# A hybrid decoder layer on one core: ten gate stripes behind the attention projections, and a recurrence's second half in three slots

## The chip, the cores and the metric

The kernel runs on one core of a Trainium2 chip. The metric is the device time of one execution in microseconds, the median of a few runs. TensorE multiplies, VectorE (DVE), ScalarE (ACT) and GpSimd (POOL) work on tiles in on-chip memory, and SyncE (SP) issues every DMA of the kernel. Each engine takes its instructions in the order in which the program wrote them.

## The reference, cut to what matters

One layer for a prompt of 1024 tokens and 8 single sample tokens, 1032 columns in all, in f32:

```
xn   = rms_norm(x, norm_pre)
u, z_rnn, q, k, v, z_attn, g_rnn, g_attn = split(xn @ w_in)      # w_in: 1024 x 9216
uc   = causal_conv(u, width 4)
r, i = sigmoid(uc @ w_a + b_a), sigmoid(uc @ w_x + b_x)           # 16 blocks of 64
a    = exp(-8 r softplus(-lambda));  b = sqrt(1 - a^2) * i * uc
h_t  = a_t h_(t-1) + b_t
y_rnn  = (h * silu(z_rnn)) @ w_rnn_out
o_g, lse_g = dilated_window_attention(q_g, k_g, v_g)              # 3 groups x 8 heads of 64
y_attn = (softmax-weighted sum of o_g * silu(z_attn)) @ w_attn_out
out  = x + rms_norm((sigmoid(g_rnn) y_rnn + sigmoid(g_attn) y_attn) @ w_out, norm_post)
```

The new convolution rows, recurrent states and keys and values are outputs too.

## The kernel before, in words

Channels lie on the 128 partitions and tokens along the row. An f32 product is made of three passes over values split into a high and a low part (`mm3`): ACT rounds the high part, DVE subtracts to get the low one. A **stripe** is 128 output channels for all 1032 tokens: four chunks of 256 to 264 columns, 8 blocks of input channels, three passes, 96 matmuls (`project`). A **pair** makes two stripes at once by a scheme of seven block products in place of eight (`project_pair`): 7 products x 2 halves x 4 blocks x 3 passes of 260 columns, with sums and differences of the weight blocks made on the fly (`pair_pieces`) and the results added up on DVE (L639). When a pair's results are complete, a close (`later(2500, ...)`, L661 and L666) copies or activates them and sends them to DRAM.

The order of the stages: norm and the first eight stripes (`FIRST`); sixteen pairs (`PAIRS`: inputs u, gates g and z, a, values v); then for four head pairs and three groups the stripes of keys and queries, with attention run between them; then eight gate stripes (`LATE_GATES`); then the output products. The last two gate stripes are written only when all merging and sampling has been written (the `until` in the loop over the late gates); `split_ya` (L1412) then splits the attention result for the next product.

What is written between the matmuls is decided by a plan. It keeps a clock `clk` in ns that only matmuls advance (a 256-column pass counts 256/2.25 + 4 ns; vector and scalar work and DMAs count nothing). Generators in named **lanes** yield a delay; `tick`, called each half chunk, runs a lane's next step when its due time is past. `later(delay, fn)` puts a call in a queue. `force` jumps the clock to the next due step where something must be finished. So delays are not waits on the chip: they set where in each engine's order an instruction stands.

Tiles come from an arena of 45 slots (`Arena`), handed out in the order in which they were freed. A slot may be freed as soon as the DMA that reads it is written; the next user then waits on the chip for that DMA. A `Room` takes a number of slots for itself. A weight load or a sample's cache load goes ahead only with some slots to spare.

The recurrence has a first half for each of eight blocks (`lru_front`: convolution and gates, run in lane `lru` beside the pairs, in a room of five slots), which stores two tiles to DRAM, and a second half (`lru_back`: loads them, tanh, exp and square root on ACT, products on DVE and POOL, a scan on DVE, the product with z on POOL, a store). The second halves run beside attention in two lanes, `lru` and `lru2`, with a room of four slots each. `attention(g, hp)` has six steps `STEP` = 3400 apart; `merge(hp)` combines the three groups by way of DRAM (L1247, L1253) and POOL (L1262 to L1267); `sample(hp)` attends for the 8 sample tokens.

Of the kernel before, what the change touches and what calls it, by code (L numbers as in the profile page):

```python
# [28 lines left out]
NSLOT = 45  # L29
WARM, WARM_STEP = 46, 7  # L30
GATES = [(kind, b) for kind in range(2) for b in range(8)]
LATE_GATES = 8


FIRST = [("u", 0), ("u", 1), ("g", 0), ("g", 1), ("z", 0), ("z", 1), ("u", 2), ("u", 3)]
PAIRS = [("u", 4), ("g", 2), ("u", 6), ("z", 2), ("v", 0), ("g", 4), ("v", 4), ("z", 4), ("v", 8), ("g", 6),
         ("a", 0), ("z", 6), ("v", 2), ("a", 2), ("v", 6), ("v", 10)]

HALF = 520
OPS = 4  # L40
STEP = 3400
SPARE = 5
KY, VY = 3000, 4000
SLOPES = [[2.0 ** (-8.0 * (g * 8 + h + 1) / 24.0) for h in range(8)] for g in range(3)]
# [52 lines left out]
def hybrid_step(ctx: ExitStack, tc: tile.TileContext, I, O):  # L97
# [10 lines left out]


    MODES = {"wide": {"pj": (0, 1, 2, 3), "s": (4, 5, 6), "o": (7,)},  # L110
             "pair": {"c": (0, 2, 6), "s": (4, 5)},
             "attention": {"pj": (0, 1), "pt": (2, 3), "s": (4, 5, 6), "o": (7,)}}
    mode, turns = ["wide"], {}
    banks = psum.tile([128, 8, 512], F32, name="banks")
# [12 lines left out]
    def later(delay, fn):  # L127
        waiting.append((clk[0] + delay, fn))
# [491 lines left out]
    def project_pair(close, last=False):  # L620

        i = W.use_pair()
        ta = new([128, 2, HALF], F32, "qa")
        quarter = lambda t, q: t[:, q].rearrange("p (c n) -> p c n", c=2)
        c11, c22 = quarter(ta, 0), quarter(ta, 1)
        for step, (wname, xname) in enumerate(STEPS):
            w = W.op(i, wname)
            if step == 1:
                tb = new([128, 2, HALF], F32, "qb")
                c21, c12 = quarter(tb, 0), quarter(tb, 1)  # L630
            p2 = ps_tile("c", 2)[:, :, :HALF // 2]
            for c in range(2):
                for k in range(4):
                    x = x_op(xname, k)[:, :, HALF // 2 * c:HALF // 2 * (c + 1)]
                    mm3(p2[:, c], w[:, 0, k], w[:, 1, k], x[:, 0], x[:, 1], k == 0, k == 3)
                    if k % 2:
                        W.work()
                        yield None
            add = lambda to, by: nc.vector.tensor_tensor(to, p2, by, op=OP.add)  # L639
            if step == 0:  # L640
                nc.scalar.activation(c11, p2, AF.Copy)
            elif step == 1:
                add(c12, c11)
            elif step == 2:
                add(c21, c12)
            elif step == 3:
                add(c12, c12)
                add(c22, c21)
            elif step == 4:
                add(c11, c11)  # L650
            elif step == 5:
                add(c21, c21)
            else:
                add(c12, c12)
            yield None
            W.drop(i, wname)
            if last and step == 3:
                for k in range(4):
                    ar.free(SX.pop(("s1", k)))
                spawn("sums", x21_back())  # L660
            if step == 4:  # L661
                later(2500, lambda: close(((0, 0, ta[:, 0]), (1, 1, ta[:, 1])), ta))
        W.pieces.pop(i)
        W.ops.pop(i)
        W.made.pop(i)
        later(2500, lambda: close(((0, 1, tb[:, 0]), (1, 0, tb[:, 1])), tb))  # L666

    def leave(dst, quarters, t, width=NT, then=None):

# [217 lines left out]
    def lru_front(b):  # L887

        while ("u", b) not in kept_uz:
            yield 1000  # L890
        L = room["L"]
        e, r, x = L(0, [128, EXT]), L(1, [128, CV]), L(2, [128, NT])
        lw = lws.pop(b) if b else load_lw(0)
        nc.sync.dma_start(e[:, 3:3 + SEQ], ud[b])
        nc.gpsimd.memset(e[:, 0:3], 0.0)
        nc.gpsimd.tensor_copy(e[:, SEQ + 6:EXT:4], us[:, b])
        nc.gpsimd.tensor_copy(e[:, SEQ + 3:].rearrange("p (b j) -> p b j", j=4)[:, :, 0:3],
                              par[:, b, 8:32].rearrange("p (b j) -> p b j", j=3))
        yield 6000
        lw = lw.rearrange("p s g c -> p (s g c)")  # L900
        lh = small.tile([128, 256], F32R, tag="lh", name="lh", bufs=1)
        ll = low_w[0]
        nc.scalar.activation(lh, lw, AF.Copy)
        for q in range(2):
            rows, ws = slice(64 * q, 64 * q + 64), slice(128 * q, 128 * q + 128)
            nc.vector.tensor_tensor(ll[rows, ws], lw[rows, ws], f32(lh[rows, ws]), op=OP.subtract)
        nc.scalar.activation(r, e[:, 0:CV], AF.Identity, scale=pcol(b, 0), bias=pcol(b, 4))
        yield 1000
        nc.vector.scalar_tensor_tensor(r, e[:, 1:1 + CV], pcol(b, 1), r, op0=OP.mult, op1=OP.add)
        nc.vector.scalar_tensor_tensor(r, e[:, 2:2 + CV], pcol(b, 2), r, op0=OP.mult, op1=OP.add)  # L910
        yield 3000
        nc.vector.scalar_tensor_tensor(x[:, :SEQ], e[:, 3:3 + SEQ], pcol(b, 3), r[:, :SEQ], op0=OP.mult, op1=OP.add)
        nc.vector.scalar_tensor_tensor(x[:, SEQ:], e[:, SEQ + 6:EXT:4], pcol(b, 3), r[:, SEQ + 3:CV:4],
                                       op0=OP.mult, op1=OP.add)
        nc.gpsimd.tensor_copy(cst[:, b, 0:3], e[:, SEQ:SEQ + 3])
        nc.gpsimd.tensor_copy(cst[:, b, 3:11], e[:, SEQ + 6:EXT:4])
        yield 2500
        xs = [L(q, [128, NT], F32R) for q in range(2)]
        a, t = L(3, [128, NT]), L(4, [128, NT])
        for q in range(2):  # L920
            rows, other = slice(64 * q, 64 * q + 64), slice(64 - 64 * q, 128 - 64 * q)
            nc.scalar.activation(xs[q][rows], x[rows], AF.Copy)
            nc.vector.tensor_tensor(xs[q][other], x[rows], f32(xs[q][rows]), op=OP.subtract)
        yield 4000
        if b + 1 < KB:
            load_lw(b + 1)
        yield 4500
        for q in range(2):
            rows = slice(64 * q, 64 * q + 64)
            ws = slice(128 * q, 128 * q + 128)  # L930
            for c0, n in CHUNKS:
                p = ps_tile("s")
                cs = slice(c0, c0 + n)
                mm(p[:, :n], lh[:, ws], xs[q][:, cs], start=True, stop=False)
                mm(p[:, :n], ll[:, ws], xs[q][:, cs], start=False, stop=True)
                for gate in range(2):
                    at = 64 * (gate ^ q)
                    nc.scalar.activation((a, t)[gate][rows, cs], p[at:at + 64, :n], AF.Sigmoid,  # L938
                                         bias=par[rows, b, 5 + gate:6 + gate])
                yield 1800  # L940
        nc.gpsimd.tensor_tensor(x, x, t, op=OP.mult)
        yield 6000
        nc.sync.dma_start(rxd[b, 0], a)
        nc.sync.dma_start(rxd[b, 1], x)

    def lru_back(b, own):
        L = room[own]
        L.shrink(4)
        a, x, t, s = (L(j, [128, NT]) for j in range(4))
        nc.sync.dma_start(a, rxd[b, 0])  # L950
        nc.sync.dma_start(x, rxd[b, 1])
        yield 8000
        nc.scalar.activation(t, a, AF.Tanh, scale=spk[:, 0, b:b + 1])
        nc.scalar.activation(a, a, AF.Exp, scale=spk[:, 1, b:b + 1])
        nc.scalar.activation(s, t, AF.Sqrt)
        yield 5000
        nc.vector.scalar_tensor_tensor(t, a, 1.0, t, op0=OP.add, op1=OP.mult)
        yield 2000
        nc.vector.tensor_scalar(t, t, -1.0, 1.0, op0=OP.mult, op1=OP.add)
        yield 2000  # L960
        nc.vector.scalar_tensor_tensor(s, t, 1.0, s, op0=OP.add, op1=OP.mult)
        yield 2500
        nc.gpsimd.tensor_tensor(s, s, x, op=OP.mult)
        z = L(0, [128, NT])
        nc.sync.dma_start(z, zd[b])
        yield 5000
        nc.vector.tensor_tensor_scan(x[:, :SEQ], t[:, :SEQ], s[:, :SEQ], 0.0, op0=OP.mult, op1=OP.add)
        nc.vector.tensor_tensor(x[:, SEQ:], t[:, SEQ:], par[:, b, 32:40], op=OP.mult)
        nc.vector.tensor_tensor(x[:, SEQ:], x[:, SEQ:], s[:, SEQ:], op=OP.add)
        nc.gpsimd.tensor_copy(cst[:, b, 11:20], x[:, SEQ - 1:])  # L970
        yield 4500
        nc.gpsimd.tensor_tensor(x, x, z, op=OP.mult)
        yield 7000
        nc.sync.dma_start(hzd[b], x)

    def state_out():
        st = new([20, D], F32, "st")
# [542 lines left out]
        spawn("lru", lru_front(b))  # L1520

    def lru_end(own):
        room[own].close()
        yield 0

    for q, (what, i) in enumerate(PAIRS):
        advance(project_pair(pair_of(what, i), last=q == len(PAIRS) - 1))
        if q == 1:
            C = late_consts()
    ar.free(*(SX.pop((q, k)) for q in ("s2", "s3", "s4") for k in range(4)))  # L1530
    room["L2"] = Room(ar, 4)
    for b in range(KB):
        spawn(("lru", "lru2")[b % 2], lru_back(b, ("L", "L2")[b % 2]))
    spawn("lru", lru_end("L"))
# [221 lines left out]
```

## Time and profile before

| | |
|---|---|
| median of 3 runs | 1279.73 us (1278.7 to 1280.13) |
| profiled execution | 1278.47 us, its span 1276.7 us |
| mean granted TensorE clock | 0.982 |
| PE busy | 1221.2 us, 96% |
| DVE, ACT, POOL busy | 756.2 us (59%), 599.7 us (47%), 261.6 us (20%) |
| HBM read and written | 122.67 and 50.45 MB |

Busy times are shares of the span from the first to the last instruction. An idle stretch in front of an instruction is put down to the instruction or DMA whose signal came last. A releaser that ended long before points to something else that held the engine up, often a DMA.

### The profile page before, as it was taken

Reading aid. Unit: us, or ns where it says so; the run is one execution under the profiler, and the core shown is the slowest. Engines: PE = TensorE matmul, PEld = TensorE weight load, DVE = VectorE, ACT = ScalarE, POOL = GpSimd, SP = SyncE. Lnnn points to the kernel's source line nnn. Section 1 sums busy time; section 2 is a strip of 40 time slices with the busy share of each in tenths; the row PEclk is TensorE's granted clock in tenths of the full one; section 3 lists DMA queues with packets and bytes.
Section 4 is the critical chain, followed back from the end, with each engine's and each line's share of the span. In section 5 each row is a group of like instructions: output and inputs, shape, how many; then the busy total and the mean of one; then the engine's idle time right before and its main releaser. Section 6 shows DMA issues by size and latency. Waiting matters only on the chain. (4 is left out here: it accounts for less than half of the span.)

```text
span 1276.7 us, 24741 instructions
## 1 busy us (share of the span) xinstructions
PE 1221.2 (96%) x9949; PEld 1176.2 (92%) x9949; DVE 756.2 (59%) x1575; ACT 599.7 (47%) x1271; POOL 261.6 (20%) x280
## 2 busy tenths in 40 slices
PE   8999999999999978999799999899999979999997
PEld 8999999999999978899788989898999979999997
DVE  5558796777686653567477464555444545545226
ACT  7634445646545556756465343343568332222222
POOL 3011042102031201122224505310422210002001
PEclk9999999999999989999899999999999989999999
DMA  8053153436434294354653853651286466313105
GB/s 254 18 174 112 39 186 117 145 113 173 129 112 146 67 257 122 133 176 139 190 161 121 223 154 87 176 139 36 70 231 182 110 240 206 93 55 116 51 18 199
DMA packets 191161, 174.67 MB, mean 137 GB/s; under 512 B 55177, under 2 KB 162665, under 8 KB 191038
## 3 DMA queue, kind: packets, MB, share of 16 engines
q1 hardware_dynamic: 191046, 173.08, 44.5%
q8 instruction: 78, 1.28, 0.4%
q14 instruction: 37, 0.30, 0.1%
HBM read 122.67 MB, written 50.45 MB: 136 GB/s over the span
## 5 line engine op out<-in xcount | busy, mean ns | idle before, releaser
L183 PE MATMUL banks<-x,whi 128*128 128x256 f32 (+1 forms) x2048 | 386.5, 289 | 5.7 <-DVE qb L639 5.7
L183 PEld LDWEIGHTS banks<-x,whi 128*128 128x128 f32 x2048 | 320.1, 192 | 11.9 <-issue 10.6
L183 PE MATMUL banks<-x,wlo 128*128 128x256 f32 (+1 forms) x1024 | 290.6, 284 | 0.2 <-DVE wlo L334 0.2
L183 PE MATMUL banks<-s,wop 128*128 128x260 f32 x1536 | 197.7, 286 | 7.2 <-DVE wop L298 4.3
L183 PEld LDWEIGHTS banks<-s,wop 128*128 128x128 f32 x1536 | 192.1, 191 | 8.6 <-DVE wop L298 5.1
L183 PEld LDWEIGHTS banks<-x,wlo 128*128 128x128 f32 x1024 | 195.6, 191 | 0.4 <-DVE wlo L334 0.4
L275 DVE TENSOR_TENSOR wlo<-wraw,whi 128x512 fp32r<-128x512 f32 x112 | 93.6, 837 | 120.6 <-ACT whi L274 101.0
L183 PE MATMUL banks<-x,wop 128*128 128x260 f32 x1152 | 146.0, 282 | 0.3 <-DVE wop L298 0.2
L183 PEld LDWEIGHTS banks<-x,wop 128*128 128x128 f32 x1152 | 142.0, 188 | 0.7 <-DVE wop L298 0.7
L1139 ACT ACTIVATE P<-P,stat 128x128 f32<-128x128 f32 (+1 forms) x192 | 84.4, 441 | 70.3 <-DVE stat L1135 70.2
L183 PE MATMUL banks<-x1b,whi 128*128 128x264 f32 (+1 forms) x512 | 101.0, 294 | 16.4 <-ACT sg L1427 7.3
L183 PEld LDWEIGHTS banks<-x1b,whi 128*128 128x128 f32 x512 | 82.1, 196 | 18.8 <-ACT sg L1427 7.5
L183 PE MATMUL banks<-wlo,mh 128*128 128x256 f32 (+1 forms) x288 | 78.8, 280 | 0.0
L183 PE MATMUL banks<-x1b,wlo 128*128 128x256 f32 (+1 forms) x256 | 74.4, 290 | 0.0
L274 ACT ACTIVATE whi<-wraw 128x512 fp32r<-128x512 f32 x112 | 68.5, 621 | 12.4 <-DMA wraw<-in_w_in 10.8
L938 ACT ACTIVATE room<-banks,par 64x256 f32<-64x256 f32 (+2 forms) x96 | 52.2, 544 | 46.2 <-PE banks L183 45.0
L183 PE MATMUL banks<-whi,ml 128*128 128x256 f32 x256 | 71.9, 281 | 0.0
L183 PE MATMUL banks<-whi,mh 128*128 128x256 f32 x256 | 71.8, 280 | 0.0
L1135 DVE CUSTOM_DVE_ANT_0 P<-banks,base 128x128 f32<-128x128 f32 (+1 forms) x192 | 56.0, 348 | 17.4 <-PE banks L183 17.3
L294 ACT ACTIVATE wop<-wsum 128x512 fp32r<-128x512 f32 x48 | 30.1, 627 | 72.9 <-DVE wsum L301 59.3
L183 PE MATMUL banks<-hzh,wlo 128*128 128x256 f32 (+2 forms) x192 | 61.3, 319 | 0.0
L183 PE MATMUL banks<-hzl,whi 128*128 128x256 f32 (+2 forms) x192 | 61.3, 319 | 0.0
(280 smaller groups left out, 2270.5 us busy)
## 6 DMA issues: line engine op xcount, KB each, us to landing
wraw<-in_w_in SPq DMA_DIRECT2D x72, 512.0 KB
ck<-in_cache_kv_w SPq DMA_DIRECT2D x24, 512.0 KB
rxd<-room SPq DMA_DIRECT2D x16, 516.0 KB
room<-rxd SPq DMA_DIRECT2D x16, 516.0 KB
sgl<-sgd SPq DMA_DIRECT2D x16, 516.0 KB
xin<-in_x_prompt SPq DMA_DIRECT2D x16, 512.0 KB
vd<-vo SPq DMA_DIRECT2D x24, 256.0 KB
vt<-vd SPq DMA_DIRECT2D x12, 512.0 KB
```

Of the source, the lines that this page charges most:

```text
L183: nc.tensor.matmul(out, lhsT, rhs, start=start, stop=stop)
L274: nc.scalar.activation(hi[:, a:b], raw[:, a:b], AF.Copy)
L275: nc.vector.tensor_tensor(lo[:, a:b], raw[:, a:b], f32(hi[:, a:b]), op=OP.subtract)
L294: nc.scalar.activation(w[:, 0], src, AF.Copy)
L938: nc.scalar.activation((a, t)[gate][rows, cs], p[at:at + 64, :n], AF.Sigmoid, bias=par[rows, b, 5 + gate:6 + gate])
L1135: nc.vector.tensor_tensor_reduce(out=pt[:, h, :128 * n], in0=ps[h][:, off:off + 128 * n], in1=base, scale=-SLOPES[g][2 * hp + h] * DIL[g], ...
L1139: nc.scalar.activation(pt[:, h, :128 * n], pt[:, h, :128 * n], AF.Exp, scale=-1.0, bias=st[:, g, 0, h, b:b + 1], accum_out=st[:, g, 1, h, ...
```

## The change

- `LATE_GATES` is 10 in place of 8, and the pair `("g", 6)` leaves `PAIRS`: two gate stripes that were a pair are now two stripes behind the keys and queries. The `until` stands ahead of the last two, as before.
- `STEP` is 3000 in place of 3400.
- The closes of a pair come 4000 in place of 2500 after its additions, and the products take the bank pairs in the order 2, 6, 0 in place of 0, 2, 6.
- `lru_front` takes its tile x later, and its two stores are put off by 5000 with `later`, where it waited 6000 itself; it ends 1000 later.
- `lru_back` works in three slots in place of four (`Room(ar, 3)`, `L.shrink(3)`): products are made in place, the square root comes after the first DVE product, two slots change places from block to block, z is loaded after the scan, and the store is put off with `later`.
- `lru_end` waits 8000 before it gives a room's slots back.

```diff
-LATE_GATES = 8
+LATE_GATES = 10
-PAIRS = [("u", 4), ("g", 2), ("u", 6), ("z", 2), ("v", 0), ("g", 4), ("v", 4), ("z", 4), ("v", 8), ("g", 6),
+PAIRS = [("u", 4), ("g", 2), ("u", 6), ("z", 2), ("v", 0), ("g", 4), ("v", 4), ("z", 4), ("v", 8),
-STEP = 3400
+STEP = 3000
-             "pair": {"c": (0, 2, 6), "s": (4, 5)},
+             "pair": {"c": (2, 6, 0), "s": (4, 5)},
-                later(2500, lambda: close(((0, 0, ta[:, 0]), (1, 1, ta[:, 1])), ta))
+                later(4000, lambda: close(((0, 0, ta[:, 0]), (1, 1, ta[:, 1])), ta))
-        later(2500, lambda: close(((0, 1, tb[:, 0]), (1, 0, tb[:, 1])), tb))
+        later(4000, lambda: close(((0, 1, tb[:, 0]), (1, 0, tb[:, 1])), tb))
...
-        yield 6000
-        nc.sync.dma_start(rxd[b, 0], a)
-        nc.sync.dma_start(rxd[b, 1], x)
+
+        def spill():
+            nc.sync.dma_start(rxd[b, 0], a)
+            nc.sync.dma_start(rxd[b, 1], x)
+        later(5000, spill)
+        yield 1000
+
+    turn = {}
 
     def lru_back(b, own):
         L = room[own]
-        L.shrink(4)
-        a, x, t, s = (L(j, [128, NT]) for j in range(4))
+        L.shrink(3)
+        turn[own] = 3 - turn.get(own, 2)
+        first, second = turn[own], 3 - turn[own]
+        a, x = L(0, [128, NT]), L(first, [128, NT])
         nc.sync.dma_start(a, rxd[b, 0])
         nc.sync.dma_start(x, rxd[b, 1])
         yield 8000
-        nc.scalar.activation(t, a, AF.Tanh, scale=spk[:, 0, b:b + 1])
+        s = L(second, [128, NT])
+        nc.scalar.activation(s, a, AF.Tanh, scale=spk[:, 0, b:b + 1])
         nc.scalar.activation(a, a, AF.Exp, scale=spk[:, 1, b:b + 1])
-        nc.scalar.activation(s, t, AF.Sqrt)
-        yield 5000
-        nc.vector.scalar_tensor_tensor(t, a, 1.0, t, op0=OP.add, op1=OP.mult)
+        yield 3500
+        nc.vector.scalar_tensor_tensor(a, a, 1.0, s, op0=OP.add, op1=OP.mult)
         yield 2000
-        nc.vector.tensor_scalar(t, t, -1.0, 1.0, op0=OP.mult, op1=OP.add)
-        yield 2000
-        nc.vector.scalar_tensor_tensor(s, t, 1.0, s, op0=OP.add, op1=OP.mult)
+        nc.scalar.activation(s, s, AF.Sqrt)
+        nc.vector.tensor_scalar(a, a, -1.0, 1.0, op0=OP.mult, op1=OP.add)
+        yield 3000
+        nc.vector.scalar_tensor_tensor(s, a, 1.0, s, op0=OP.add, op1=OP.mult)
         yield 2500
         nc.gpsimd.tensor_tensor(s, s, x, op=OP.mult)
-        z = L(0, [128, NT])
+        yield 5000
+        nc.vector.tensor_tensor_scan(x[:, :SEQ], a[:, :SEQ], s[:, :SEQ], 0.0, op0=OP.mult, op1=OP.add)
...
+        yield 4000
+        z = L(second, [128, NT])
         nc.sync.dma_start(z, zd[b])
         yield 5000
...
         nc.gpsimd.tensor_tensor(x, x, z, op=OP.mult)
-        yield 7000
-        nc.sync.dma_start(hzd[b], x)
+        later(7000, lambda: nc.sync.dma_start(hzd[b], x))
...
     def lru_end(own):
+        yield 8000
         room[own].close()
-        yield 0
...
-    room["L2"] = Room(ar, 4)
+    room["L2"] = Room(ar, 3)
```

## Rows read from the trace of the kernel before

**Rows 1.** Stages: window, length, busy us (count) by engine, PEclk, DMA, GB/s.

```profile
118.00:466.80 348.80, 341.29 (x2774) 339.24 (x2773) 256.94 (x365) 181.11 (x285) 68.52 (x140) 0.99 0.40 129
466.80:905.60 438.80, 411.36 (x3514) 379.50 (x3515) 252.88 (x672) 222.92 (x556) 118.29 (x59) 0.97 0.52 145
1001.60:1035.00 33.40, 26.14 (x205) 25.93 (x204) 13.67 (x23) 7.93 (x17) 15.13 (x6) 0.90 0.46 131
```

**Rows 2.** TensorE's timeline: start, length, instruction, [idle before it and what ended it].

```profile
363.77 4.44 PE L183 MATMUL banks<-s,wop 128*128 128x260 f32 x22 [1.93 <-DVE wop L298]
...
472.41 0.77 PE L183 MATMUL banks<-x,whi 128*128 128x256 f32 x2 [5.65 <-DVE qb L639]
...
496.25 0.50 PE L183 MATMUL banks<-x1b,whi 128*128 128x256 f32 x2 [2.97 <-ACT qt L1022]
...
618.85 0.80 PE L183 MATMUL banks<-x1b,whi 128*128 128x256 f32 x2 [5.85 <-DVE kt L1026]
...
643.61 0.81 PE L187 MATMUL banks<-ident,sc 128*64 128x128 f32 x3 [3.09 <-DVE stat L1135]
...
806.37 0.27 PE L187 MATMUL banks<-ident,qn 128*24 128x128 f32 x1 [3.68 <-DVE stat L1135]
...
1028.97 0.81 PE L183 MATMUL banks<-x1b,whi 128*128 128x264 f32 x2 [7.26 <-ACT sg L1427]
```

**Rows 3.** Busy time by stretch: behind a stall, one gate stripe, clean pairs.

```profile
618.80:623.30 4.50, 4.45 (x21) 4.45 (x22) 1.36 (x3) 0.00 (x0) 0.00 (x0) 0.51 0.82 268
1001.57:1013.04 11.47, 11.47 (x99) 11.47 (x97) 5.28 (x14) 2.35 (x5) 0.78 (x1) 1.00 0.71 173
250.00:275.00 25.00, 25.00 (x210) 25.00 (x209) 16.19 (x25) 12.66 (x18) 3.76 (x8) 1.00 0.54 177
```

**Rows 4.** Timeline of SP, POOL and ACT at the last merge.

```profile
1002.49 0.32 SPq L1247 DMA_DIRECT2D fd<-ft  x1
...
1012.26 7.13 POOL L1262 TENSOR_TENSOR ot<-ot,fb 128x1024 f32<-128x1024 f32 x3 [28.07 <-DMA fb<-fd]
...
1015.41 1.07 ACT L1412 ACTIVATE yah<-ot 128x1024 fp32r<-128x1024 f32 x1 [7.54 <-DMA out_kv_s<-sr]
...
1027.58 1.06 ACT L1412 ACTIVATE yah<-ot 128x1024 fp32r<-128x1024 f32 x1 [10.84 <-POOL ot L1267]
```

**Rows 5.** TensorE's timeline: the scores of two attention steps in a row.

```profile
925.20 0.93 PE L183 MATMUL banks<-kt,qt 64*128 64x128 f32 x8
...
931.54 0.93 PE L183 MATMUL banks<-kt,qt 64*128 64x128 f32 x8
```

**Rows 6.** Line 907, once in each first half: count, ns min/median/max, first and last start.

```profile
L907 ACT ACTIVATE room<-room,par x8: 1256/1262/1274, 123.1 to 456.6; 128x1056 f32<-128x1056 f32 x8
```

**Rows 7.** DVE's timeline at the end of the pairs.

```profile
468.44 2.49 DVE L923 TENSOR_TENSOR room<-room,room 64x1032 fp32r<-64x1032 f32 x2 [3.00 <-ACT room L922]
...
470.96 1.31 DVE L639 TENSOR_TENSOR qb<-banks,qb 128x520 f32<-128x520 f32 x2
```

**Rows 8.** ACT's timeline at the first second half.

```profile
490.32 1.28 ACT L955 ACT_TABLE_LOAD   x1
491.61 1.07 ACT L955 ACTIVATE room<-room 128x1032 f32<-128x1032 f32 x1
...
493.22 1.28 ACT L938 ACT_TABLE_LOAD   x1
```

**Rows 9.** Timeline of SP and DVE at the stall before 618.85.

```profile
606.86 7.17 SPq L1097 DMA_DIRECT2D out_kv_p<-kn  x4
...
617.61 0.69 DVE L275 TENSOR_TENSOR wlo<-wraw,whi 128x512 fp32r<-128x512 f32 x1 [11.20 <-DMA out_kv_p<-kn]
```

**Rows 10.** SP's waits: total us, times, longest.

```profile
SPq L965 <- DVE room L957: 54.4, 7, 16.4
```

**Rows 11.** ACT's timeline in the pairs, at the stall before 363.77.

```profile
355.75 1.07 ACT L847 ACTIVATE zo<-qb 128x1040 f32<-128x1040 f32 x1 [3.85 <-DVE qb L639]
...
360.54 0.64 ACT L294 ACTIVATE wop<-wsum 128x512 fp32r<-128x512 f32 x1 [1.76 <-DMA zad<-qa]
```

More of the change, by code (lines that the diff above doesn't have):

```diff
@@ L891, in lru_front @@
         L = room["L"]
-        e, r, x = L(0, [128, EXT]), L(1, [128, CV]), L(2, [128, NT])
+        e, r = L(0, [128, EXT]), L(1, [128, CV])
         lw = lws.pop(b) if b else load_lw(0)
@@ L911, in lru_front @@
         yield 3000
+        x = L(2, [128, NT])
         nc.vector.scalar_tensor_tensor(x[:, :SEQ], e[:, 3:3 + SEQ], pcol(b, 3), r[:, :SEQ], op0=OP.mult, op1=OP.add)
@@ L952, in lru_back @@
         yield 8000
-        nc.scalar.activation(t, a, AF.Tanh, scale=spk[:, 0, b:b + 1])
+        s = L(second, [128, NT])
+        nc.scalar.activation(s, a, AF.Tanh, scale=spk[:, 0, b:b + 1])
         nc.scalar.activation(a, a, AF.Exp, scale=spk[:, 1, b:b + 1])
-        nc.scalar.activation(s, t, AF.Sqrt)
-        yield 5000
-        nc.vector.scalar_tensor_tensor(t, a, 1.0, t, op0=OP.add, op1=OP.mult)
+        yield 3500
+        nc.vector.scalar_tensor_tensor(a, a, 1.0, s, op0=OP.add, op1=OP.mult)
         yield 2000
-        nc.vector.tensor_scalar(t, t, -1.0, 1.0, op0=OP.mult, op1=OP.add)
-        yield 2000
-        nc.vector.scalar_tensor_tensor(s, t, 1.0, s, op0=OP.add, op1=OP.mult)
+        nc.scalar.activation(s, s, AF.Sqrt)
+        nc.vector.tensor_scalar(a, a, -1.0, 1.0, op0=OP.mult, op1=OP.add)
+        yield 3000
+        nc.vector.scalar_tensor_tensor(s, a, 1.0, s, op0=OP.add, op1=OP.mult)
         yield 2500
         nc.gpsimd.tensor_tensor(s, s, x, op=OP.mult)
-        z = L(0, [128, NT])
+        yield 5000
+        nc.vector.tensor_tensor_scan(x[:, :SEQ], a[:, :SEQ], s[:, :SEQ], 0.0, op0=OP.mult, op1=OP.add)
+        nc.vector.tensor_tensor(x[:, SEQ:], a[:, SEQ:], par[:, b, 32:40], op=OP.mult)
+        nc.vector.tensor_tensor(x[:, SEQ:], x[:, SEQ:], s[:, SEQ:], op=OP.add)
+        nc.gpsimd.tensor_copy(cst[:, b, 11:20], x[:, SEQ - 1:])
+        yield 4000
+        z = L(second, [128, NT])
         nc.sync.dma_start(z, zd[b])
         yield 5000
[L967 to L971, printed above, removed]
         nc.gpsimd.tensor_tensor(x, x, z, op=OP.mult)
-        yield 7000
-        nc.sync.dma_start(hzd[b], x)
+        later(7000, lambda: nc.sync.dma_start(hzd[b], x))
     def state_out():
```

## The prediction, made before the changed kernel was built or run

> **What bounds the kernel now.** I read the stages first, in the table of busy time by stretch. TensorE is busy 341.3 of 348.8 us while the pairs run, 411.4 of 438.8 us in the attention stage, and 26.1 of 33.4 us under the last two gate stripes [rows 1]. DVE, the next engine, stays under 75% and under 60%. So TensorE's order is the bound, and the time can move only by its work or its stalls. The timeline of TensorE alone gives the stalls; the seven that I use are in [rows 2], each with its length and the instruction that ended it. After each long one the records show the lower level, 1.2 GHz, for a while: in the 4.5 us behind the stall before 618.85 the mean grant is 0.51, and 21 matmuls take what 37 take at 0.12 us each [rows 3]. I price that at 1.9 us behind a stall of over 5 us, and at 1.6 us behind one of about 3 us (between nothing and 1.9).
>
> The sum is made against the profiled execution, 1278.47 us (its span of 1276.7 and 1.8 around it); the median of the runs is 1279.73, 1.26 more.
>
> **Part 1, the pair that becomes two stripes.** A pair issues 7 products x 2 halves x 12 = 168 matmuls; the clean stretch of the pair stage runs 210 in 25 us, so 20.0 us. A gate stripe takes 11.47 us [rows 3]. Two less one pair: 22.9 - 20.0 = **+2.9 us** of TensorE work, with little doubt (2.6 to 3.2). The pair's 14 roundings on ACT, 13 subtractions and 6 additions on DVE go, and 4 and 4 halves of a stripe's weights come; both engines have room. The weights' loads and the gates' stores keep their bytes and move to the end of SP's queue.
>
> **Part 2, the end of attention.** The last two gate stripes start only when the order has everything of merging and sampling behind it. Here that point is 1001.57 us, and the last merge is then forced out at once: its store leaves at 1002.49, its factors are back at 1012.26, POOL needs until 1027.58 for six products and sums, and `split_ya` (L1412) holds ACT for 7.54 us (a slot whose store is still going out) and then 10.84 us for POOL. Gate evacuations stand behind it on ACT, TensorE runs out of banks and waits 7.26 us [rows 2, 4]. The chain is 25 us and has 22.9 us of stripes, cut by a blocked ACT. With ten stripes the point comes two stripes, 22.9 us, later, while the chain starts where attention ends: 25 - 22.9 = 2 us are left, and the fourth split is 3 x 1500 ns behind the first. So this wait should go: -7.26 - 1.9 = **-9.2 us** (to 0 if attention itself comes later). What is late next is the first weight of the attention output, which has two more stripes to arrive in.
>
> **Part 3, attention steps.** A step may be due 3000 instead of 3400 ns of the plan's clock after the one before, but the plan looks only every half chunk, and a half chunk counts 12 x 118 = 1413 ns. Two make 2827: short of both numbers, so the third decides in both cases. The trace has the steps at 925.20 and 931.54, 6.3 us apart: three half chunks (4.3 us) and the step's own work [rows 5]. Only where another lane adds between 173 and 573 ns of matmuls does a step move, about one for each head pair. I take **0** (four half chunks, 6 us, sooner at the end at most).
>
> **Part 4, the recurrence.** (a) A first half now ends 1000 instead of 6000 ns after its last product, the two stores put off by 5000. Eight first halves start 47.6 us apart (333.5/7) [rows 6], the last at 456.6, and it straddles the end of the pairs: DVE waits 3.0 us for ACT's half of a split, and the last pair's addition behind it ends at 472.3, for which TensorE waited 5.65 us [rows 2, 7]. Seven times 5 us sooner, against pairs that end 20 us sooner, puts that split 15 us ahead of the end. An addition (0.7 us) and its signals stay: -(5.65 - 1.0) - 1.9 = **-6.6 us** (0 to -7.6). (b) The same half's gate sigmoids meet the first second half on ACT at 490 to 495: a table load for the root, another for the sigmoid, 1.28 us each, and TensorE waited 2.97 us for a query evacuation behind them [rows 2, 8]. The sigmoids would be gone: -4.6 with its slow stretch at best, **-3** taken. (c) The root is split from tanh and exp, so ACT is held for 2.4 us at a time and not 4.7 (two passes of about 1.1 us; the load of 1.28 and the root's pass of 1.07 [rows 8]). The chunk that two banks hide takes 11.47/4 = 2.9 us. The stall before 643.61 is of that kind: -4.7 at best, **-2** taken. (d) Three slots in each room leave two more for all else. A weight split waited 11.2 us on DVE for a slot whose key store took 7.17 us to issue, and TensorE 5.85 us [rows 2, 9]. Freed slots queue, so two more free ones put such a reuse later, yet samples and weight loads that wait for slots take them up: between 0 and -7.8, **-4** taken. (e) The load of z is issued behind the scan, and SP waits in order: today it stands 54.4 us in all, in 7 waits, for its slot at that load [rows 10]. Weights, cache and value loads queue behind. The wait may grow or shrink by the same; 0 taken, -5 to +5 kept.
>
> **Part 5, closes put off from 2500 to 4000.** Now ACT's sigmoid of an a pair waits 3.85 us for DVE's last addition; that goes. But the tile's store leaves 1.5 us later, and a weight rounding that took its slot already waits 1.76 us for it [rows 11]. The stall before 363.77 came from both, and one more like it. Between -6.6 (both stalls with slow stretches) and +6; **0** taken. The other bank order of the products moves nothing: no row shows a wait at the first pair.
>
> **New stalls.** Stalls outside those named, such as 3.68 us before 806.37, come from what happens to meet, and every meeting moves. The attention stage has 27.4 us of them, 17.6 named; of the 9.8 left I let under half come anew: **+4** (0 to +10).
>
> Sum: +2.9 - 9.2 - 6.6 - 3 - 2 - 4 + 4 = -17.9, so 1260.6 by the profiled run, about **1262 us** by the median.
>
> A rule of the Trainium skill speaks against part 4c. ScalarE: Activation LUTs, section "Table sets: the hidden batching unit", wants calls batched by table set; its section "What ACT_TABLE_LOAD costs" prices a switch at about 2.66 us with its drain, where the rows show 1.28 us for the load alone. Without the split of the root as a gain the sum would be 2 us higher; the rival built on the rule stands below.
>
> **Rivals.** (1) The stalls change place: TensorE loses as much elsewhere as the named ones give back. For it: each comes from a meeting within 3 us, and all meetings shift. Against: two of them have a cause that the change takes away. Time: 1278 to 1282, no change. (2) Slower: closes hold two tiles 1.5 us longer in a stage where slots decide, so weight operands come late. 30 closes x 1.5 = 45 us at most; it turns the sign once 12 of them (17.9/1.5) reach TensorE in full. Half with 1.6 us of slow clock at seven: 22.5 + 11.2 - 17.9 = +16, 1296 us. Against: the pair stage loses only 7.5 us today. (3) Each root now stands between another lane's exponentials, and loads double: 8 x 2 x 1.28 = 20.5 us of ACT, in full on the path, and the 2 us of part 4c lost: 20.5 + 2 - 17.9 = +4.6, 1284 us. This is the page's rule as a mechanism here. Against: the eight roots have a load each already (one of them stands in [rows 8]), tanh and exp still go out together, and ACT is half idle there. (4) The change does not do what it says for the steps, as part 3 has it; that they close up after all would give no other time, for part 2 has its gain already. Both lie within the forecast.
>
> **How the numbers follow.** Forecast 0.77, rival 1 0.11, rival 2 0.09, rival 3 0.03. 0.2% is about what a measurement of this kernel can tell from no change, so faster 0.77, same 0.11, slower 0.12. The named gains at their best with no new stall give 2.9 - 9.2 - 7.6 - 4.6 - 4.7 - 7.8 = -31, 1249 us, and part of the closes' gain brings the lower end to 1246. Parts 4d, 4b and 4c at nothing and new stalls of 10 us give 1277, and rival 1 brings the upper end to 1281. Range 1246 to 1281.
>
> **What would show it.** Right: pairs end near 447 us; no wait over 1.5 us at the first key stripe; `split_ya` finds its products ready; attention steps still 6 us apart; eight loads for the root. Wrong: a wait of ACT for POOL at the last gates, stalls in the pairs on a slot's store, or the attention stage losing 27 us again under other names.

## The result, and the profile after

The changed kernel takes 1264.59 us (median of 4 runs, 1264.04 to 1266.06) where the kernel before took 1279.84 beside it: a ratio of 0.9884, interval 0.9867 to 0.9901. The profiled execution takes 1264.04 us with a span of 1262.2, 14.4 us less than the one before. The forecast was 1262 us, within 1246 to 1281.

The first view is the busy time by stretch of the kernel after, with the columns of [rows 1]: from the first pair to the first key matmul, to the last query evacuation, to the first matmul of the attention output.

```profile
118.00:448.40 330.40, 320.35 (x2614) 318.34 (x2612) 255.28 (x352) 182.35 (x287) 73.12 (x141) 0.99 0.40 128
448.40:874.80 426.40, 411.06 (x3546) 376.99 (x3546) 258.71 (x668) 215.86 (x545) 121.90 (x61) 0.98 0.54 151
874.80:1019.70 144.90, 140.88 (x1198) 135.19 (x1199) 62.77 (x150) 73.00 (x161) 35.96 (x16) 0.98 0.49 140
```

Between the same points the kernel before needs 354.4, 433.2 and 128.1 us, and 243.0 from there to the end (now 242.5). So the pairs give 24.0 us, the stage of keys and queries 6.8, and the stage of the late gates costs 16.8. The terms of the prediction, put into these stretches, say -24.7 (a pair less, the wait at its end), -6.9 (its slow clock, 4b, 4c, 4d and the new stalls) and +13.7 (two stripes, less the wait at the end of attention). Stage by stage the sums are close; the third is 3.1 us off. The stalls beneath them, from TensorE's timeline after, to be held against [rows 2]:

```profile
448.44 0.51 PE L183 MATMUL banks<-x,whi 128*128 128x256 f32 x2 [2.55 <-DVE qb L639]
...
477.81 0.50 PE L183 MATMUL banks<-x,whi 128*128 128x256 f32 x2 [1.24 <-ACT smp L1033]
...
491.72 1.67 PE L187 MATMUL banks<-ident,P 128*128 128x128 f32 x6 [3.02 <-ACT P L1148]
...
682.74 0.27 PE L187 MATMUL banks<-ident,qn 128*24 128x128 f32 x1 [4.45 <-DVE stat L1144]
...
885.92 0.37 PE L187 MATMUL banks<-ident,qn 128*24 128x128 f32 x1 [3.36 <-DVE stat L1144]
```

The wait at the end of the pairs is down from 5.65 to 2.55 us. The one at 618 has no heir of its size, and the 7.26 us at the last gates are gone. That last one can be read at its source, in the timelines of SP, POOL and ACT at the last merge (before: [rows 4]):

```profile
964.82 0.34 SPq L1256 DMA_DIRECT2D fd<-ft  x1
...
988.02 2.72 POOL L1276 TENSOR_TENSOR ot<-ot,zal 128x1024 f32<-128x1024 f32 x1
...
997.90 1.05 ACT L1421 ACTIVATE yah<-ot 128x1024 fp32r<-128x1024 f32 x1
...
1005.91 1.05 ACT L1421 ACTIVATE yah<-ot 128x1024 fp32r<-128x1024 f32 x1
```

The factors' store leaves 38 us sooner than before, POOL has its last product at 990.7, and the four splits on ACT begin 7 us later with no idle time in front of them. The attention output's matmuls begin at 1019.7.

Three more views answer to steps of the prediction: line 907 once in each first half (as [rows 6]), the loads of the root's table, and SP's wait for z (as [rows 10]).

```profile
L907 ACT ACTIVATE room<-room,par x8: 1254/1259/1262, 122.9 to 421.6; 128x1056 f32<-128x1056 f32 x8
```

```profile
L967 ACT ACT_TABLE_LOAD  x8: 1283/1283/1283, 467.0 to 624.2; - x8
```

```profile
SPq L980 <- DVE room L976: 58.5, 7, 22.3
```

First halves start 42.7 us apart (before 47.6), the root has its eight loads, and SP stands 58.5 us where it stood 54.4.

### The profile page after: what moved, and what is told of

Same layout as the page of the kernel before. It is cut to its first block, busy times and chain, and to the rows that moved or that the text cites. A ratio compares the mean times of both kernels' runs of the same rounds, so it can differ in the third digit from the quotient of the medians.

```text
span 1262.2 us, 24783 instructions
## 1 busy us (share of the span) xinstructions
PE 1220.6 (97%) x9973; PEld 1174.5 (93%) x9973; DVE 764.2 (61%) x1561; ACT 595.9 (47%) x1270; POOL 262.2 (21%) x280
## 3 DMA queue, kind: packets, MB, share of 16 engines
q8 instruction: 78, 1.28, 0.4%
## 4 chain that ended last, share of the span: by engine, by line
PE 80%; DVE 10%; ACT 5%; issue 3%; DMA 1%; DVEq 0%; POOL 0%; ACTq 0%; SPq 0%; POOLq 0%
PE banks L183 75%; PE banks L187 5%; DVE wop L298 1%; DVE wlo L275 1%; DVE qb L639 1%; ACT P L1148 1%; ACT vo L829 1%; DVE wsum L301 1%; DVE room L974 1%; DMA rxd<-room 1%; DMA vd<-vo 1%; DVE P L1144 1%; DVE room L924 1%; DVE room L909 0%; ACT whi L274 0%
## 5 line engine op out<-in xcount | busy, mean ns | idle before, releaser
L183 PE MATMUL banks<-x,whi 128*128 128x256 f32 (+1 forms) x2144 | 401.8, 288 | 3.8 <-DVE qb L639 2.6
L183 PEld LDWEIGHTS banks<-x,whi 128*128 128x128 f32 x2144 | 332.4, 190 | 10.2 <-issue 4.8
L183 PE MATMUL banks<-x,wlo 128*128 128x256 f32 (+1 forms) x1072 | 303.1, 283 | 0.2 <-DVE wlo L334 0.2
L183 PE MATMUL banks<-s,wop 128*128 128x260 f32 x1440 | 183.8, 284 | 4.4 <-DVE wop L298 3.4
L183 PEld LDWEIGHTS banks<-s,wop 128*128 128x128 f32 x1440 | 179.1, 190 | 5.0 <-DVE wop L298 3.8
L275 DVE TENSOR_TENSOR wlo<-wraw,whi 128x512 fp32r<-128x512 f32 x116 | 103.1, 889 | 131.1 <-ACT whi L274 124.6
L183 PE MATMUL banks<-x,wop 128*128 128x260 f32 x1080 | 137.3, 283 | 3.2 <-DVE qb L639 2.5
L183 PEld LDWEIGHTS banks<-x,wop 128*128 128x128 f32 x1080 | 132.9, 188 | 4.4 <-issue 3.0
L1148 ACT ACTIVATE P<-P,stat 128x128 f32<-128x128 f32 (+1 forms) x192 | 84.2, 440 | 62.7 <-DVE stat L1144 62.6
L183 PE MATMUL banks<-x1b,wlo 128*128 128x264 f32 (+1 forms) x272 | 77.9, 286 | 0.0
L1144 DVE CUSTOM_DVE_ANT_0 P<-banks,base 128x128 f32<-128x128 f32 (+1 forms) x192 | 56.0, 347 | 23.2 <-PE banks L183 22.9
L183 PE MATMUL banks<-hzh,whi 128*128 128x256 f32 (+2 forms) x192 | 61.3, 319 | 0.0
```

Of the source, the lines that this page charges most:

```text
L183: nc.tensor.matmul(out, lhsT, rhs, start=start, stop=stop)
L275: nc.vector.tensor_tensor(lo[:, a:b], raw[:, a:b], f32(hi[:, a:b]), op=OP.subtract)
L1144: nc.vector.tensor_tensor_reduce(out=pt[:, h, :128 * n], in0=ps[h][:, off:off + 128 * n], in1=base, scale=-SLOPES[g][2 * hp + h] * DIL[g], ...
L1148: nc.scalar.activation(pt[:, h, :128 * n], pt[:, h, :128 * n], AF.Exp, scale=-1.0, bias=st[:, g, 0, h, b:b + 1], accum_out=st[:, g, 1, h, ...
```

## The experiments

Each of the four edits was tried alone on the kernel before and left out alone from the kernel after. "Effect" is (ratio - 1) x 1280 us. The last two columns are read from the timelines: from the first pair (118 us) to the last query evacuation, and from there to the first matmul of the attention output; they are of the one profiled execution, which can lie a few us off the median. The first pair begins between 117.9 and 121.1 us, because the stage ahead of it, whose program is the same in all of them, differs by as much from execution to execution; that difference is inside the first of the two columns.

| kernel | median us | ratio (interval) | effect us | to the last query | to the attention output |
|---|---|---|---|---|---|
| before | 1279.84 | 1 | 0 | 787.6 | 128.1 |
| before + gates | 1293.4 | 1.0112 (1.0081 to 1.0143) | +14.3 | 789.1 | 140.3 |
| before + recurrence | 1289.3 | 1.0073 (1.0052 to 1.0094) | +9.3 | 797.5 | 128.8 |
| before + closes | 1274.4 | 0.9962 (0.9944 to 0.9980) | -4.9 | 783.9 | 128.8 |
| before + STEP | 1272.5 | 0.9952 (0.9936 to 0.9967) | -6.1 | 797.5 | 111.4 |
| before + gates + recurrence | 1260.0 | 0.9851 (0.9806 to 0.9896) | -19.1 | 756.1 | 141.9 |
| after | 1264.59 | 0.9884 (0.9867 to 0.9901) | -14.8 | 756.8 | 144.9 |
| after without gates | 1276.8 | 0.9981 (0.9963 to 0.9999) | -2.4 | 792.7 | 124.6 |
| after without recurrence | 1283.3 | 1.0036 (1.0017 to 1.0054) | +4.6 | 787.3 | 132.0 |
| after without closes | 1265.8 | 0.9902 (0.9875 to 0.9930) | -12.5 | 762.4 | 144.7 |
| after without STEP | 1254.3 | 0.9809 (0.9784 to 0.9834) | -24.4 | 752.3 | 141.8 |

**The ten gate stripes alone, and left out.** The first is this edit on the kernel before, the second its reverse on the kernel after:

```diff
-LATE_GATES = 8
+LATE_GATES = 10
-PAIRS = [..., ("v", 8), ("g", 6), ...
+PAIRS = [..., ("v", 8), ...
```

> The kernel before with only the gates moved: fifteen pairs, ten late stripes. Theory: the wait of 7.3 us at the last stripe goes with its slow clock, 2.9 us of work come; the pairs end 20 us sooner and so 20 us ahead of the last first half, whose split no longer stands before the last addition, so the 5.65 us at the first key stripe shrink to under 2: 1267 to 1274, 1270. Rival (stalls change place): 1276 to 1283.

> The changed kernel with eight late gate stripes and sixteen pairs again, all else changed. Theory (the last two stripes need two more ahead of them to cover the last merge): ACT waits for the last POOL product again, TensorE stalls 5 to 8 us at the last gate stripe, with 1.9 us of slow clock, and 2.9 us of work go: 1271 us (1268 to 1274). Rival (stalls only change place): within 4 us of 1264.6, and no such wait need appear.

Alone it costs 14.3 us; taken out of the whole change it costs 12.4. Neither time lies where the theory or the rival put it. Alone, the tail does what part 2 says: 140.3 is 128.1 + 22.9 - 10.7, and the 7.26 us wait is gone. The loss lies before: the pairs end 29.6 us sooner, but the stage of keys and queries takes 464.3 us in place of 433.2, of which TensorE stands 42.5 and not 21.8, and its mean grant is 0.95 and not 0.97. The last first half still stores at 507.6, now 65 us behind the end of the pairs and not 31, so more of its work on DVE and ACT falls into the next stage, and the last second half stores at 718.5 (before 696.4). The longest new stall, in TensorE's, DVE's, SP's and POOL's timelines of this kernel:

```profile
724.79 1.22 PE L183 MATMUL banks<-kt,qt 64*128 64x128 f32 x6 [10.13 <-DVE st L982]
```

```profile
718.48 1.25 DVE L1079 STREAM_TRANSPOSE kn<-kt 128x1024 f32<-128x1024 f32 x1 [8.43 <-POOL room L972]
...
721.46 2.25 DVE L275 TENSOR_TENSOR wlo<-wraw,whi 128x512 fp32r<-128x512 f32 x1 [1.73 <-DMA hzd<-room]
```

```profile
718.47 0.33 SPq L974 DMA_DIRECT2D hzd<-room  x1
```

```profile
709.09 7.04 POOL L1262 TENSOR_TENSOR ot<-ot,fb 128x1024 f32<-128x1024 f32 x3
716.09 2.36 POOL L972 TENSOR_TENSOR room<-room,room 128x1032 f32<-128x1032 f32 x1
```

The last block's product with z stands on POOL behind three products of a merge. DVE waits 8.43 us for it, SP has its store only then, and a weight split waits for that store: 10.13 us of TensorE, from a second half that is late enough to meet the merge. What DVE waits for are the last reader and the store of a room's slot, and here `lru_end` gives the room back as soon as that store is written; the change lets it wait 8000 first, which was not run by itself.

Taken out of the whole change, the wait at the last gate stripe comes back only as 2.08 us, not as the 5 to 8 expected, although ACT stands 10.43 us for POOL's last product there. TensorE's timeline of that kernel:

```profile
1032.27 0.51 PE L183 MATMUL banks<-x1b,whi 128*128 128x264 f32 x2 [2.08 <-ACT sg L1436]
```

What that kernel loses lies mostly in the stage of keys and queries: 437.9 us in place of 426.4 in the kernel after, with 7.63 us before 701.34 as the longest stall.

**The recurrence alone, and left out.** The edit is the diff of `lru_front`, `lru_back`, `lru_end` and the room of three.

> The kernel before with only the recurrence changed. Theory: the stall at the first key stripe goes (6.6 us with its slow clock), those behind slots and behind tanh, exp and root shrink by 9; the wait at the last gate stripe stays: 1266 us (1262 to 1271). Rival (stalls change place): 1276 to 1283.

> The changed kernel with the recurrence of before (first half waits 6000 itself, second half in four slots, its stores waited for). Theory: the end of attention stays covered, but the waits for slots and the long hold of ACT by tanh, exp and root come back in the attention stage: 1270 us (1267 to 1275), the stage losing 20 us or more to stalls. Rival (stalls only change place): 1260 to 1268, the stage's loss unchanged.

Alone it costs 9.3 us, left out it costs 19.4; both times are above every range that was given for them. Alone, the end of attention keeps its wait and the pairs get new ones (TensorE's timeline):

```profile
394.31 4.43 PE L183 MATMUL banks<-s,wop 128*128 128x260 f32 x22 [4.30 <-DVE wop L298]
...
1039.80 0.81 PE L183 MATMUL banks<-x1b,whi 128*128 128x264 f32 x2 [7.24 <-ACT sg L1436]
```

The pairs take 362.3 us, 7.9 more than before. Ahead of 394.31 a first half's split of x (L923 on ACT from 389.36 to 391.49, L924 on DVE from 390.44 to 392.92) stands before a weight's rounding and subtraction; the other new waits were not read. Left out of the change, the picture of the gates alone comes back: the last first half stores at 503.1, the last second half at 709.4, and the longest stall stands behind a weight's rounding on ACT that waits for POOL's merge. TensorE and ACT in the kernel after without the recurrence's edit:

```profile
750.61 1.67 PE L187 MATMUL banks<-ident,P 128*128 128x128 f32 x6 [9.97 <-ACT P L1139]
```

```profile
746.58 0.63 ACT L274 ACTIVATE whi<-wraw 128x512 fp32r<-128x512 f32 x1 [14.68 <-POOL ot L1262]
```

**Both together.** Alone the two cost 23.6 us; if they were independent the pair of them would be slower than the kernel before.

> The kernel before with the gates moved and the recurrence changed, closes and attention steps as before. Alone the one cost 14 us and the other 9. Theory (they need each other: fifteen pairs want first halves that end with them, and rooms that hold fewer slots beside the attention that then starts sooner): 1252 to 1262, below the whole change. Rival (costs and gains add up): 1280 plus 14 plus 9, above 1290.

They give 19.1 us, with neither the closes nor STEP: 42.7 us better than the sum of the two. With the recurrence's edit the last first half stores at about 464 us and the last second half at 654, and the shortened pair stage is a gain instead of work pushed into attention. That the two edits need each other is shown; which part of the recurrence's edit the gates need is tried next.

**Which half of the recurrence's edit.** Two kernels each undo a part of it in the kernel after. Four slots in a room, of which three are used:

```diff
-        L.shrink(3)
+        L.shrink(4)
-    room["L2"] = Room(ar, 3)
+    room["L2"] = Room(ar, 4)
```

> The changed kernel with rooms that hold four slots again, of which the second half still uses three: two slots less for all else, nothing else edited. Theory (the slots are what the recurrence's part brings): 1272 to 1290, with stalls over 5 us behind instructions that wait for the last reader of a slot, and the attention stage losing over 20 us. Rival (its order and its early end bring it): within 4 us of 1264.6.

And the first half with its old end:

```diff
-        def spill():
-            nc.sync.dma_start(rxd[b, 0], a)
-            nc.sync.dma_start(rxd[b, 1], x)
-        later(5000, spill)
-        yield 1000
+        yield 6000
+        nc.sync.dma_start(rxd[b, 0], a)
+        nc.sync.dma_start(rxd[b, 1], x)
```

> The changed kernel with first halves that wait 6000 and then store, as before. Theory (early end matters because a first half that outlasts the pairs holds five slots and meets the first key stripes): last first half 35 us later and past the end of the pairs, 1270 to 1280. Rival (slots of the rooms alone): within 4 us of 1264.6.

The slots are worth 9.1 us (1273.7; ratio 0.9955, 0.9937 to 0.9972), the first halves' end 5.6 (1270.4; 0.9928, 0.9907 to 0.9950): 14.7 of the 19.4, if the two add up, which no run tells. With the first halves late again the last one stores at 504.9 us, 62.6 behind the end of the pairs, as with the gates alone; yet that kernel is 9.2 us faster than the one before. So late first halves by themselves are not what makes the gates cost 14.3 us alone. With four slots held, weights come late: ACT's waits for a weight's load (total us, times, longest) in the kernel after and in the one with four slots, then TensorE, ACT and SP in the latter.

```profile
ACT whi L274 <- DMA wraw<-in_w_in: 6.1, 4, 2.5
```

```profile
ACT whi L274 <- DMA wraw<-in_w_in: 21.5, 6, 6.7
```

```profile
601.85 1.11 PE L187 MATMUL banks<-ident,vt 128*128 128x128 f32 x4 [7.13 <-DVE pick L1230]
```

```profile
597.21 0.63 ACT L274 ACTIVATE whi<-wraw 128x512 fp32r<-128x512 f32 x1 [6.71 <-DMA wraw<-in_w_in]
```

```profile
587.29 0.32 SPq L980 DMA_DIRECT2D room<-zd  x1
...
588.66 0.54 SPq L259 DMA_DIRECT2D wraw<-in_w_in  x1
```

The weight's load is issued at 588.66, behind the load of z on SP, and TensorE waits 7.13 us. So part 4d has a real size. The split of the root, the later load of z and the wait of 8000 in `lru_end` were not run by themselves.

**The closes alone, and left out.**

```diff
-                later(2500, lambda: close(...
+                later(4000, lambda: close(...
-             "pair": {"c": (0, 2, 6), "s": (4, 5)},
+             "pair": {"c": (2, 6, 0), "s": (4, 5)},
```

> The kernel before with only the closes at 4000 and the bank order 2, 6, 0. Theory: the waits of ACT for a pair's last addition go, a wait for a store takes their place, 1280 within 4 us. Rival 2 (slots): 1284 or more, with more stalls in the pairs. Third reading (ACT freed): 1274 or less, the stalls before 363.8 and 430.2 gone.

> The changed kernel with closes at 2500 and the bank order 0, 2, 6. Theory (what ACT no longer waits for DVE, a slot waits for its store): within 3 us of 1264.6. Rival 2 (later closes cost slots): faster, below 1261, with fewer stalls in the pairs. A third reading (later closes free ACT): above 1268, with waits of ACT for the last additions back.

Alone -4.9 us, between the range of the theory and that of the third reading: the pair stage falls from 354.4 to 348.3, and the stall before 363.77 [rows 2] and its like at 430 are gone. Left out of the change, 2.3 us with intervals that overlap: not told from nothing. The cost that I held against it, the stores 1.5 us later, shows nowhere: ACT's waits for stores at a weight's rounding in the pairs (L294) fall from 11.9 to 2.7 us in all.

**STEP alone, and left out.**

```diff
-STEP = 3400
+STEP = 3000
```

> The kernel before with only the attention steps due 3000 apart. Theory (three half chunks either way): 1280 within 3 us, the same stalls. Rival (closer steps end attention sooner): 1275 or less, with a shorter wait at the last gate stripe.

> The changed kernel with attention steps due 3400 apart. Theory (the plan looks only each half chunk, so three half chunks either way): within 2 us of 1264.6, steps still 6 us apart, attention ending 1 to 6 us later. Rival (closer steps bring the end of attention nearer and cover it): 1268 or more, with a wait at the last gate stripes.

Alone it gives 6.1 us; within the change it costs 9.6. This is the step of the prediction that failed, and it failed in both directions: the theory missed both times, and the rival held alone but not within the change. The steps are as far apart as forecast, as TensorE's timeline after shows, against [rows 5]:

```profile
925.03 0.71 PE L183 MATMUL banks<-kt,qt 64*128 64x128 f32 x8
931.32 0.72 PE L183 MATMUL banks<-kt,qt 64*128 64x128 f32 x8
937.41 0.71 PE L183 MATMUL banks<-kt,qt 64*128 64x128 f32 x8
```

But some head pairs do gain a half chunk or more. Alone on the kernel before, the last scores start at 963.2 us and not 975.1 (TensorE's timeline, before and with STEP alone):

```profile
975.09 0.71 PE L183 MATMUL banks<-kt,qt 64*128 64x128 f32 x8
```

```profile
963.24 0.72 PE L183 MATMUL banks<-kt,qt 64*128 64x128 f32 x8
```

Those 12 us cover most of the chain of the last merge, and the 7.26 us wait goes by this edit too. The two columns of the table, +9.9 and -16.7 us, are mostly attention work that moved ahead of the last query: TensorE is busy 10.3 us longer in the first and 9.2 shorter in the second. With ten stripes that wait is covered already, and the last step at 937.41 in place of 939.79 is worth nothing. What is left is the other effect: the steps stand elsewhere against the rest. The stretches of the kernel after without it:

```profile
449.70:870.30 420.60, 405.77 (x3506) 372.08 (x3507) 256.67 (x667) 214.18 (x543) 116.52 (x58) 0.99 0.55 153
870.30:1012.10 141.80, 141.58 (x1239) 135.31 (x1238) 61.14 (x151) 76.77 (x165) 44.28 (x19) 1.00 0.51 145
```

Of 7.5 us between the two profiled executions, 5.8 lie in the stage of keys and queries and 3.1 in the tail, where 141.80 is 128.1 + 22.9 - 9.2, parts 1 and 2 (the first stretch goes 1.3 the other way, with a first pair that begins 2.6 us later). The tail's 3.1 us go with the stall before 885.92; without the edit no wait there is over 0.25 us.

**POOL's sums cut in two.** That stall and the ones at 682.74 (after) and 806.37 (before, [rows 2]) end in the same instruction: the softmax statistics on DVE, ahead of a sample's query. The timelines of DVE ahead of 885.92, of DVE and POOL ahead of 806.37 in the kernel before, and ahead of its heir in the kernel after without STEP, which TensorE's timeline puts at 3.69 us:

```profile
878.48 2.68 DVE L275 TENSOR_TENSOR wlo<-wraw,whi 128x512 fp32r<-128x512 f32 x1 [1.01 <-ACT whi L274]
881.08 2.32 DVE L1300 TENSOR_TENSOR n<-smp 128x24 f32<-128x24 f32 x1
```

```profile
798.59 2.68 DVE L275 TENSOR_TENSOR wlo<-wraw,whi 128x512 fp32r<-128x512 f32 x1 [1.02 <-ACT whi L274]
801.19 2.32 DVE L1291 TENSOR_TENSOR n<-smp 128x24 f32<-128x24 f32 x1
...
804.17 0.68 DVE L275 TENSOR_TENSOR wlo<-wraw,whi 128x512 fp32r<-128x512 f32 x1
```

```profile
798.32 2.40 POOL L1265 TENSOR_TENSOR ot<-ot,ot 128x1024 f32<-128x1024 f32 x1
800.80 2.67 POOL L1267 TENSOR_TENSOR ot<-ot,zal 128x1024 f32<-128x1024 f32 x1
```

```profile
764.91 2.68 DVE L275 TENSOR_TENSOR wlo<-wraw,whi 128x512 fp32r<-128x512 f32 x1 [1.01 <-ACT whi L274]
767.51 2.32 DVE L1300 TENSOR_TENSOR n<-smp 128x24 f32<-128x24 f32 x1
...
772.69 0.31 PE L187 MATMUL banks<-ident,qn 128*24 128x128 f32 x1 [3.69 <-DVE stat L1144]
```

The same split takes 2.68 us while POOL has a sum of 2.40 us going, and 0.68 us when POOL is idle. A product of 24 columns takes 2.32. The whole of these traces says the same. Of the splits in the kernels before, after and after without STEP, 41 take over 0.9 us: each of them begins while a two-operand instruction of POOL runs, and ends 0.54 to 0.55 us behind that instruction's end. The product of 24 columns takes 0.17 to 0.18 us where POOL runs none as it begins (twice before, all four times with STEP alone, which has no stall of this kind). Elsewhere (twice before, four times after, four times after without STEP) it ends 0.04 us behind the one that runs, and takes 1.9 to 2.4 us. That is waiting for a turn, not a shared rate. If the two-operand instruction on DVE stands until POOL's current one ends, shorter ones on POOL bound the wait. The kernel after without STEP, with each large two-operand instruction of POOL issued in two halves:

```diff
+    def pool_mul(o, x, y, op=OP.mult):
+        n = o.shape[1] // 2
+        for c in (slice(0, n), slice(n, 2 * n)):
+            nc.gpsimd.tensor_tensor(o[:, c], x[:, c], y[:, c], op=op)
...
-        nc.gpsimd.tensor_tensor(y, y, o1, op=OP.add)
+        pool_mul(y, y, o1, OP.add)
```

> The changed kernel with attention steps due 3400 apart, and every large product or sum of POOL cut into two halves. Theory (a two-tensor operation of DVE stands until the POOL operation of the moment ends, so 0.69 us become up to 2.9): DVE's slowed splits fall to 1.9 us at most, the stall of 3.7 us before a sample's first transposition to 2 or less, time 1247 to 1253 against 1254.3. Rival (the slowing is by share, not by turn, or POOL's own end decides): within 2 us of 1254.3 or above.

1248.7 us (1248.4 to 1249.2), ratio 0.9762 (0.9726 to 0.9799): the fastest of all, 31 us under the kernel before and 16 under the changed one. The interval touches that of the kernel after without STEP (0.9784 to 0.9834), but all four of its runs lie under all four of the other's (1253.4 to 1256.4). The same place on DVE and TensorE, and the splits of the whole run without and with halves (count, total us, mean ns of one, idle before them):

```profile
758.60 1.60 DVE L280 TENSOR_TENSOR wlo<-wraw,whi 128x512 fp32r<-128x512 f32 x1 [1.02 <-ACT whi L279]
760.13 1.25 DVE L1305 TENSOR_TENSOR n<-smp 128x24 f32<-128x24 f32 x1
...
764.63 0.27 PE L187 MATMUL banks<-ident,qn 128*24 128x128 f32 x1 [1.93 <-DVE stat L1149]
```

```profile
L275 DVE TENSOR_TENSOR wlo<-wraw,whi 128x512 fp32r<-128x512 f32 x116 | 103.1, 889 | 133.0 <-ACT whi L274 130.6
```

```profile
L280 DVE TENSOR_TENSOR wlo<-wraw,whi 128x512 fp32r<-128x512 f32 x116 | 92.0, 794 | 141.6 <-ACT whi L279 139.1
```

The stall is 1.93 us where it was 3.69, the splits take 11 us less, and the run 5.6. No split takes over 1.9 us now. The stall shown is only a part of the gain: of 8.0 us between the two profiled executions, 2.4 lie ahead of the first pair, 2.8 in the pairs and 2.8 in the stage of keys and queries.

## Why the prediction was right, and where it was not

- **What bounds it:** right. TensorE's busy time is 1220.6 us after and 1221.2 before; of the 14.4 us between the two spans 13.9 are its stalls, and the slow clock that goes pays for the work that comes.
- **Parts 1 and 2:** right in size where the steps are 3400 apart. +22.9 - 9.2 is found to 0.1 us in the tail of the kernel without STEP (141.8), and in 141.9 with gates and recurrence alone. In the whole change the 9.2 us are not the gates' own: with steps 3000 apart and eight stripes the wait is 2.08 us already, and the 12.4 us that the gates are worth there lie mostly in the stage of keys and queries, where I had no term for them. What the step left out is that a pair that goes takes cover from the recurrence: its price on its own is +14.3 us, not -6.3. What the cover consists of is open in part; the first halves' earlier end is worth 5.6 us. The remark on a pair's work beside TensorE is wrong and changes no term: the trace has 7 roundings, 11 subtractions and 7 additions for each pair (112, 176 and 112 for sixteen), not 14, 13 and 6.
- **Part 3:** failed. I took 0 because steps stay 6 us apart, which they do. But I bounded what the rare step that closes up can bring by 6 us at the end. Alone it is 11.9 us there and -6.1 us in all, since the merge's chain starts there; in company that gain is covered, as rival 4 has it. And I did not price what a moved step meets: +9.6 us in company.
- **Part 4a:** right in mechanism, mis-sized: 5.65 to 2.55 us and the slow stretch with it, some 5 us of the 6.6, and the 2.55 us are over the 1.5 that I had named as a sign. The split that I named is clear of the end; in its place DVE waits 3.94 us for ACT's rounding of x (L607), which stands behind copies of values and the last first half's sigmoids.
- **Part 4b:** wrong. The stall before 496.25 went, and one of 3.02 us stands before 491.72: ACT waits there 4.36 us for DVE, which has a second half's scan (2.26 us) ahead, and then loads a table (1.28). With the 1.24 before 477.81 nothing is gained where I had -3.
- **Part 4c:** the stall before 643.61 is gone, but nothing separates the split root from the slots: open.
- **Part 4d:** right in kind, mis-sized: 9.1 us in company against -4 (0 to -7.8).
- **Part 4e:** SP's wait for z is 58.5 us, 4.1 more; my range of 5 was one of time, and what these 4.1 us cost TensorE no run separates.
- **Part 5:** -4.9 alone, -2.3 at best in company; the 0 was the middle of a range that held both.
- **New stalls:** 4.45 and 3.36 us of one kind where I had +4 (0 to +10), and the kind could have been read: it stands in [rows 2] as the stall before 806.37, which I called "what happens to meet". The Trainium skill has it. SBUF — State Buffer, section "Who interferes with whom", says that a DVE instruction with two inputs in SBUF contends with a GpSimd instruction that reads SBUF, and its section "Summary: rules for kernel authors" says that the second to issue is held until the first is done. The rows agree (2.68 us beside POOL, 0.68 alone). I had not weighed it, though a moved attention step moves what meets on the two engines; how much of the +9.6 us of STEP comes by it no run separates.
- **Rivals:** stalls that change place (1) are half of the truth in the attention stage; 4b is one. Closes that hold tiles (2) are refuted by the run with closes alone. Of doubled table loads (3) there are none: eight for the root, and 42 in all against 45. The page of the Trainium skill behind it (ScalarE: Activation LUTs, section "Table sets: the hidden batching unit") asks for batching by table set; here splitting the root from its batch added no load, because each root had one before.

So the total was right within 2.6 us by terms of which several were wrong apart; that their errors met is luck. The sum treated four edits as independent; measured alone they add up to +12.6 us, and together they give -14.8. The terms are prices in company: 4a, for one, counts on first halves and pairs that both end sooner. Against leaving out, the recurrence was forecast at -15.6 (4a to 4d) and is worth -19.4, gates -6.3 and -12.4, closes 0 and -2.3, STEP 0 and +9.6, where my +4 for new stalls stood for all edits together. Why the recurrence brings new waits into the pairs when it stands alone stays open, as does the share of each moved instruction in the 42.7 us.

## What to carry to other kernels

Price an edit in the company in which it will run, and say which other edit gives it cover: an engine's shortened stage is worth what the work beside it can follow, here the recurrence. Whenever something is only moved, ask first what starts at its new end, and then what it meets there. Where a short two-operand instruction on DVE takes as long as the one on POOL beside it, try POOL's work in shorter instructions before anything is rescheduled.

## What was not expected of the hardware

- The wait of DVE for POOL is not idle time in the trace: it lengthens the DVE instruction itself. A product of 24 columns that takes 2.32 us in place of 0.17 is its mark. Copies of 256 columns out of the banks (0.42 us) and the statistics over 128 (0.28 us) keep their time beside POOL.
- TensorE's granted clock fell with no idle time before it. In these two stretches of the kernel after TensorE is busy throughout; in the first the grant is 1.00 (2.4 GHz), in the second 0.62, so for most of it 1.2 GHz:

```profile
668.00:672.00 4.00, 4.00 (x41) 3.69 (x39) 0.43 (x1) 1.10 (x1) 4.00 (x3) 1.00 0.83 252
672.00:676.50 4.50, 4.50 (x26) 4.50 (x27) 3.84 (x3) 0.63 (x1) 4.50 (x2) 0.62 0.76 209
```

What TensorE did just before is its timeline's next row, sixteen of the matmuls with a single column that sum a sample's weighted values:

```profile
670.61 1.95 PE L183 MATMUL banks<-one,ck 128*128 128x1 f32 x16
```

Each run has four such groups. In the kernel after, the one at 759.90 has a fall behind it too (mean grant 0.50 from 761.7 to 765.0, with 0.45 us of idle time ahead of the group); those at 850.5 and 961.95 have none. In the kernel after without the gates and in the kernel before with the recurrence alone the grant also falls to 0.50 (at 792.7 and 715.4) right behind such a group, with TensorE busy throughout the group. So it is no single coincidence; but the group does not bring the fall each time, and what decides it no run here shows.
